# Opening an output projection with its ready tiles, and placing three root broadcasts later, in a two-layer decoder trunk

## The chip, the cores and the metric

The kernel runs on one core of one Trainium2 chip. The metric is the time of one execution on the device, in microseconds; less is better. It is written with a tile framework that places the semaphores. The order of TensorE's instructions is the order in which the program issues them; the other engines' orders are chosen by the framework's scheduler.

## The reference, cut to what matters

A trunk of two layers works on 528 tokens (16 meta tokens and 512 others) of width 1024, in float32. Each layer is a SwiGLU feed-forward block at half weight, a token mixer, and a second feed-forward block; layer 0 mixes by gated linear attention, layer 1 by sliding-window attention on a shared key/value set.

```python
def swiglu(x, w_in, w_out):
    gate, up = jnp.split(x @ w_in, 2, axis=-1)
    return (jax.nn.silu(gate) * up) @ w_out

# gated linear attention, end: o is the attention's output, (tokens, 4 heads, 256)
o = rmsnorm(o, g_head) * jax.nn.silu(r).reshape(B, L, GLA_HEADS, GLA_DV)
return o.reshape(B, L, GLA_V) @ w_out

# trunk, per layer
h = h + 0.5 * rmsnorm(swiglu(rmsnorm(h, g[0]), w_ffn_in[layer, 0], w_ffn_out[layer, 0]), g[1])
h = h + rmsnorm(mix, g[3])
h = h + 0.5 * rmsnorm(swiglu(rmsnorm(h, g[4]), w_ffn_in[layer, 1], w_ffn_out[layer, 1]), g[5])
```

The hidden width of a feed-forward block is 2816, that is 22 tiles of 128. Each head of the linear attention is normalized by its own root of mean square over its 256 channels.

## The kernel before

Activations lie transposed: 128 channels on the partitions, tokens along the free axis. Layer 0 works on two groups of tokens, of 272 and 256; most of layer 1's feed-forward work takes one group of 512. Each float32 operand is split into a high and a low part in a reduced format (ScalarE copies the high part, VectorE subtracts to get the low one), and each product is three matmuls: high by high, low by high, high by low (`mm3s`).

**A feed-forward block** (`ffn`) goes through its 22 hidden tiles in four chunks, of 4, 6, 6 and 6 (`FF_CHUNKS`). The first chunk is plain: `x_first` and `x_units` compute gate and up for four tiles, `evac` multiplies them and splits each into a pair tile `hid...` (L642 to L647, then L411 for the high and L412 for the low part). Then `out_proj` multiplies the four hidden tiles by the output weights: for each of eight output tiles m and each token group, four hidden tiles by three matmuls go into one PSUM bank `y`, which ScalarE copies to `Y` (L587). The later chunks use Strassen's scheme and begin their output projection early: `out_steps` is a generator that has a path for that, taken when it is given a list of `jobs` (evacuations still under way). There `begin` issues the matmuls of all hidden tiles but the last for the first output units, then the jobs are awaited, then `unit` adds the last hidden tile and evacuates. Meanwhile `right_factors` prepares the Strassen operands (`z...`, `xs...`) on ScalarE and VectorE.

**The linear attention** (`gla`) issues projections unit by unit through `x_units` (48 matmuls a unit with both groups), and between them the steps of one head at a time, `core(h, ...)`. A head begins when the head before it has ended: it waits for `cores[h - 1 : h]`. Its first step on TensorE transposes the values (`pv`). At its end the squares of its output are summed by matmuls with a vector of ones (`st_go`), GpSimd finds the reciprocal root by a chain of small operations and spreads it on a diagonal (`dg_go`, L387), two pairs of matmuls broadcast the diagonal to all partitions (`r_go`), and VectorE scales the head's output in `Y` (L987). This is `rstd`, called from `scale`, once per token group. The last eight projections are gates: `gated` (L1003 to L1010, then L411 and L412) needs the scaled output and makes the pair tiles `og`, which the attention's output projection reads; gates 0 and 1 wait for head 0, gates 2 and 3 for head 1, gates 4 to 7 for head 3.

**The order** is set by a planner, `Flow`. It keeps a clock that advances with each matmul by its columns over 2400 us (600 for plain float32). Side work is written as generators; `yield d` puts the rest of one back until the planner's clock has advanced by d, and it is issued when the matmuls of the main line have come that far (`flow.pump` after each product). So a number after `yield` says how many matmuls stand in TensorE's order between two steps. `rstd` yields `CHAIN + more` (5.0 plus what the caller asks for) between the sums and the broadcast; `BEHIND` is 2.2. `flow.wait(job)` issues side work until that job has ended.

**Weights** come by DMA on SyncE's queue into eight raw buffers; their splits go into the pool of 32 pair tiles (`SLOTS`), which also holds operands, hidden tiles and the tiles of the linear attention. `set_ahead` limits how many of them weights may hold; `done_w` gives them back when a unit of work has used them, and lets the next load go.

Of the kernel before, what the change touches and what calls it, by code (L numbers as in the profile page):

```python
# [46 lines left out]
BEHIND = 2.2  # L47
# [77 lines left out]
def trunk_kernel(ctx: ExitStack, tc, a, out):  # L125
    nc = tc.nc
    pe, act, dve, pool, sp = nc.tensor, nc.scalar, nc.vector, nc.gpsimd, nc.sync
    flow = Flow()
# [16 lines left out]
    def ps(name):  # L145
        return pp.tile([P, 512], F32, tag="ps", name=name)

    def pair_tile(name, dt=F32R):
        return hp.tile([P, 2, TOK], dt, tag="pair", name=name)

    def duo(name):
        t = pair_tile(name, F32)
        return t[:, 0], t[:, 1]
# [4 lines left out]
    def gain(layer, i, k):  # L158
        c = V_GAIN + layer * 48 + i * 8 + k
        return vec[:, c : c + 1]  # L160

    def mm(o, lhs, rhs, start=True, stop=True, onto=False):
        inst = pe.matmul(o, lhs, rhs, start=start, stop=stop, skip_group_check=onto)  # L163
        n = 1
        for d in rhs.shape[1:]:
            n *= d
        flow.clock += n / 2400 if rhs.dtype == F32R else max(n / 600, 0.12)
        return inst
# [41 lines left out]
    def set_ahead(n, slots=None):  # L210
        ahead[0], limit[0] = n, slots or n
        room[0].finish(flow)
        room[0] = Job(None)
# [138 lines left out]
    def rstd(sq, n, dim, half, name, eng=pool, more=0.0):  # L352
        c = 128 if n % 128 == 0 else n // 4
        nch = n // c
        st = ps(f"st_{name}")
        for j in range(nch):
            for i, t in enumerate(sq):
                mm(st[:c, j : j + 1], t[:, j * c : (j + 1) * c], ones[:, 0:1], i == 0, i == len(sq) - 1)
        av = sm.tile([P, 4], F32, tag="av", name=f"av_{name}")
        yv = sm.tile([P, 4], F32, tag="yv", name=f"yv_{name}")  # L360
        zv = sm.tile([P, 4], F32, tag="zv", name=f"zv_{name}")
        wv = sm.tile([P, 4], F32, tag="wv", name=f"wv_{name}")
        aa, yy, zz, ww = av[:c, :nch], yv[:c, :nch], zv[:c, :nch], wv[:c, :nch]
        if eng is dve:
            dve.tensor_scalar(aa, st[:c, :nch], 1.0 / dim, 1e-6, op0=ALU.mult, op1=ALU.add)
        else:
            act.activation(aa, st[:c, :nch], AF.Identity, scale=1.0 / dim, bias=eps[:c])
        eng.tensor_scalar(yy.bitcast(I32), aa.bitcast(I32), -0.5, RSQRT_MAGIC, op0=ALU.mult, op1=ALU.add)

        eng.tensor_tensor(zz, yy, yy, op=ALU.mult)  # L370
        eng.tensor_tensor(zz, zz, aa, op=ALU.mult)
        eng.tensor_scalar(ww, zz, 0.375, -1.25, op0=ALU.mult, op1=ALU.add)
        eng.tensor_tensor(ww, ww, zz, op=ALU.mult)
        if eng is dve:
            dve.scalar_tensor_tensor(yy, ww, 1.875, yy, op0=ALU.add, op1=ALU.mult)
            dve.tensor_tensor(zz, yy, yy, op=ALU.mult)
            dve.scalar_tensor_tensor(zz, zz, -0.5, aa, op0=ALU.mult, op1=ALU.mult)
            dve.scalar_tensor_tensor(yy, zz, 1.5, yy, op0=ALU.add, op1=ALU.mult)
        else:
            pool.tensor_scalar(ww, ww, 1.875, None, op0=ALU.add)  # L380
            pool.tensor_tensor(yy, yy, ww, op=ALU.mult)
            pool.tensor_tensor(zz, yy, yy, op=ALU.mult)
            pool.tensor_tensor(zz, zz, aa, op=ALU.mult)
            pool.tensor_scalar(zz, zz, -0.5, 1.5, op0=ALU.mult, op1=ALU.add)
            pool.tensor_tensor(yy, yy, zz, op=ALU.mult)
        dg = sm.tile([P, 272], F32, tag="dg", name=f"dg_{name}", bufs=2)
        eng.tensor_tensor(  # L387
            dg[:c, :n].rearrange("p (j c) -> p j c", c=c),
            (hident if half else ident)[:c, :c].unsqueeze(1).to_broadcast([c, nch, c]),
            yy.unsqueeze(2).to_broadcast([c, nch, c]),  # L390
            op=ALU.mult,
        )
        yield (DCHAIN if eng is dve else CHAIN) + more
        r = ps(f"r_{name}")
        mm(r[:, :n], ones[:c, :], dg[:c, :n])
        return r
# [12 lines left out]
    def split(dst, src, g):  # L409
        o, n = g  # L410
        act.activation(dst[:, 0, o : o + n], src, AF.Copy)  # L411
        dve.tensor_tensor(dst[:, 1, o : o + n], src, dst[:, 0, o : o + n].bitcast(F32), op=ALU.subtract)  # L412
# [142 lines left out]
    def out_proj(*args, **named):  # L555
        for _ in out_steps(*args, **named):
            pass
# [71 lines left out]
    def ffn(x, groups, finish, opening=False, tail=4):  # L629
        set_ahead(8 if opening else 16)  # L630

        def evac_to(hids):
            gss = {}

            def evac(i, g, p):
                o, n = g
                r = x.rt[:, o : o + n]
                if i % 2 == 0:
                    if i not in gss:
                        gss[i] = duo("gu")  # L640
                    gs = gss[i][0][:, o : o + n]
                    dve.tensor_tensor(gs, p[:, :n], r, op=ALU.mult)  # L642
                    act.activation(gs, gs, AF.Silu)
                else:
                    gs, us = (t[:, o : o + n] for t in gss[i - 1])
                    dve.tensor_tensor(us, p[:, :n], r, op=ALU.mult)
                    dve.tensor_tensor(us, gs, us, op=ALU.mult)  # L647
                    split(hids[i // 2], us, g)

            return evac  # L650

        jobs = []
        n2 = sum(n for _, n in groups) // 2
        halves = [(groups[0][0], n2), (groups[0][0] + n2, n2)]
        z, plain = {}, Job(None)

        def new_hid():
            hids.append(pair_tile(f"hid{x.name}_{lo + len(hids)}"))
            return hids[-1]

        for ci, (lo, hi) in enumerate(FF_CHUNKS):
            hids = []
            if ci == 0:
                jobs = x_first(x, 4, evac_to([new_hid() for _ in range(2)]), opening)
                set_ahead(16, 4)
                factors = flow.spawn(right_factors(x, halves, z, plain))
                for t in range(2, hi):
                    jobs += x_units(x, 2, groups, evac_to([new_hid()]))
                plain.finish(flow)
                set_ahead(16, 8)  # L670
            else:
                flow.wait(factors)
                set_ahead(16, RING)
                tiles = Strassen(z, halves)
                cur = tiles.head(new_hid())
                while cur:
                    last = len(hids) == hi - lo
                    if last:
                        fin = (finish, KD, True) if lo >= LAST else (None, 0, False)
                        proj = out_steps(hids, groups, x.groups, False, *fin, jobs)  # L680
                        end = used[0] + NLAST + tail
                    tiles.body(cur, (lambda: next(proj)) if last else (lambda: None))
                    nxt = None if last else tiles.head(new_hid())
                    jobs.append(tiles.tail(cur, last))
                    cur = nxt
            if ci == 0:
                flow.wait(*jobs)
                out_proj(hids, groups, x.groups, True)
                continue
            if lo >= LAST:  # L690
                set_ahead(32)
                cap[0] = min(end, len(units))
            for _ in proj:
                pass
# [121 lines left out]
    def gla(x, finish):  # L816
        set_ahead(10)
        with tc.tile_pool(name="gp", bufs=1) as gp:
# [61 lines left out]
            def core(h, before):  # L880
# [98 lines left out]
                accs = []  # L979
# [3 lines left out]
                        square_into(accs[gi], Y[:, 2 * h + i, o : o + n], i, 2, f"go{h}_{gi}")  # L983
                yield 2.0
                def scale(gi, o, n):
                    r = yield from rstd(accs[gi], n, 256, True, f"go{h}_{gi}", more=h // 3 * BEHIND)
                    dve.tensor_tensor(  # L987
                        yy[:, :, o : o + n], yy[:, :, o : o + n],
                        r[:, :n].unsqueeze(1).to_broadcast([P, 2, n]), op=ALU.mult,
                    )  # L990
# [32 lines left out]
            jobs = []  # L1023
# [208 lines left out]
    x = Operand("l0f0", lambda k: gain(0, 0, k), L0)  # L1232
# [51 lines left out]

    nxt, fin = into("l0m", 0, 1, True, lambda k: gain(0, 2, k), L0)
    ffn(x, L0, fin, True)
    x = nxt
    nxt, fin = into("l0f1", 0, 3, False, lambda k: gain(0, 4, k), L0)
    gla(x, fin)
    x = nxt  # L1290
    nxt, fin = into("kv", 0, 5, True, lambda k: vec[:, V_KVN + k : V_KVN + k + 1], L0)
    ffn(x, L0, fin, tail=8)


    with tc.tile_pool(name="kp", bufs=1) as kp:
        x = Operand("l1f0", lambda k: gain(1, 0, k), L1)
# [10 lines left out]
        x = nxt  # L1307
# [89 lines left out]
```

## Time and profile before

| what | value |
|---|---|
| median of 3 runs | 1932.98 us (1929.79 to 1935.67) |
| the profiled execution | 1932.53 us |
| its span, first to last instruction | 1930.5 us |
| mean granted TensorE clock | 0.992 of full speed |
| VectorE, ScalarE, GpSimd busy | 74%, 52%, 12% |
| DMA, mean over the span | 90 GB/s |

The profile is of one execution. A row of a timeline has the start in us, the length in us, the engine, the line of the kernel, the operation, what it writes and reads, the count of instructions merged in it, and in brackets the idle time of the engine before it with what ended it. PE is TensorE's matmuls, PEld its weight loads, which go ahead of the matmuls; DVE is VectorE, ACT ScalarE, POOL GpSimd, SP SyncE. A matmul of 272 columns in the reduced format follows the one before it after some 0.12 us, one of 512 columns after some 0.23 us. A row of the list of waits has who waited, for whom, the total in us, how often, and the longest. A row of a table of stretches has the stretch, its length, for each engine asked for the busy time and the count of instructions, then the granted clock, the DMA engines' share and GB/s.

Places in the span, in us: the four plain chunks' output projections begin at 60, 692, 1085 and 1610; the linear attention's roots stand at 466, 503, 542 and 581, and its output projection begins at 592.

### The profile page before, as it was taken

The page shows a single profiled execution, that of the slowest core. Times are in us where ns is not written, and L with a number is a line of the kernel's source. Part 1 is how long each engine was busy: PE and PEld are TensorE (multiplying, and loading weights), DVE is VectorE, ACT ScalarE, POOL GpSimd, SP SyncE. Part 2 cuts the span into 40 slices and gives each one's busy share as a digit, 9 for nine tenths or more (in the row PEclk, how much of TensorE's full clock was granted, in tenths as well). Part 3 has the DMA queues.
Part 4 walks back from the last instruction along what each step waited for, and adds up shares of the span by engine and source line. Part 5 has one row for each costly group of instructions (what it writes and reads, how often), then busy time and mean ns, then how long its engine had stood idle before and what let it go on. Part 6 is the DMA issues. An engine that isn't in the chain of part 4 may idle for free.

```text
span 1930.5 us, 37342 instructions
## 1 busy us (share of the span) xinstructions
PE 1889.1 (98%) x14502; PEld 1801.1 (93%) x14502; DVE 1419.5 (74%) x2868; ACT 1002.5 (52%) x2268; POOL 223.0 (12%) x417
## 2 busy tenths in 40 slices
PE   8999999999999999999999999999998999999997
PEld 8999999999999999999999798989975798989897
DVE  7885858765465798586887786868779678868584
ACT  5553535653245565353574553535646565536363
POOL 2000000321121300000034000000352040000002
PEclk9999999999999999999999999999999999999998
DMA  4223233322113122333351223233321212333331
GB/s 165 91 91 107 91 106 98 123 67 77 56 45 110 56 72 90 106 91 105 99 175 45 66 83 115 91 112 102 123 66 34 69 36 85 95 107 104 105 115 44
DMA packets 102016, 174.61 MB, mean 90 GB/s; under 512 B 11344, under 2 KB 24144, under 8 KB 101840
## 3 DMA queue, kind: packets, MB, share of 16 engines
q1 hardware_dynamic: 101008, 171.59, 28.4%
q8 instruction: 113, 1.85, 0.4%
q10 hardware_dynamic: 832, 0.65, 0.1%
q14 instruction: 63, 0.52, 0.1%
HBM read 170.10 MB, written 2.10 MB: 89 GB/s over the span
## 4 chain that ended last, share of the span: by engine, by line
PE 82%; DVE 12%; ACT 3%; issue 2%; POOL 1%; DMA 0%; SPq 0%; DVEq 0%; ACTq 0%
PE y L163 30%; PE a L163 18%; PE x L163 14%; PE c L163 8%; PE d L163 4%; DVE raw L252 1%; DVE w L228 1%; ACT w_s L246 1%; DVE w_s L247 1%; DVE w L247 1%; PE e L163 1%; PE o L163 1%; PE po L163 1%; DVE xsl0f L723 0%; PE ps L163 0%
## 5 line engine op out<-in xcount | busy, mean ns | idle before, releaser
L247 DVE TENSOR_TENSOR w_s<-raw,w_s 128x512 fp32r<-128x512 f32 x288 | 194.1, 691 | 132.9 <-ACT w_s L246 131.0
L163 PE MATMUL y<-hidl0f,w 128*128 128x272 f32 (+1 forms) x2112 | 264.8, 287 | 3.3 <-ACT hidl0f L411 3.1
L163 PEld LDWEIGHTS y<-hidl0f,w 128*128 128x128 f32 x2112 | 261.7, 190 | 4.4 <-ACT hidl0f L411 3.5
L228 DVE TENSOR_TENSOR w<-raw,w 128x512 fp32r<-128x512 f32 x378 | 243.2, 674 | 17.2 <-ACT w L227 15.4
L163 PE MATMUL y<-hidl1f,w 128*128 128x512 f32 (+1 forms) x1344 | 251.1, 346 | 1.7 <-ACT hidl1f L411 1.4
L246 ACT ACTIVATE w_s<-raw 128x512 fp32r<-128x512 f32 x288 | 175.3, 628 | 145.2 <-DVE raw L252 141.5
L163 PEld LDWEIGHTS y<-hidl1f,w 128*128 128x128 f32 x1344 | 212.3, 188 | 36.6 <-ACT hidl1f L411 2.3
L227 ACT ACTIVATE w<-raw 128x512 fp32r<-128x512 f32 x378 | 208.1, 586 | 35.4 <-PE y L163 27.0
L407 POOL TENSOR_TENSOR acc_post<-acc_post,sq_post 128x256 f32<-128x256 f32 (+1 forms) x72 | 59.1, 821 | 1376.7 <-ACT sq_post L406 1376.1
L252 DVE TENSOR_TENSOR raw<-raw,raw 128x512 f32<-128x512 f32 x288 | 198.3, 688 | 5.5
L247 DVE TENSOR_TENSOR w<-raw,w 128x512 fp32r<-128x512 f32 x216 | 148.6, 688 | 39.5 <-ACT w L246 38.8
L246 ACT ACTIVATE w<-raw 128x512 fp32r<-128x512 f32 x216 | 134.0, 621 | 48.0 <-PE y L163 47.7
L163 PE MATMUL x<-x_l0m,w 128*128 128x272 f32 (+1 forms) x1200 | 158.1, 288 | 0.0
L163 PEld LDWEIGHTS x<-x_l0m,w 128*128 128x128 f32 x1200 | 149.3, 189 | 1.1
L589 DVE TENSOR_TENSOR Y<-y,Y 128x256 f32<-128x256 f32 (+2 forms) x176 | 82.5, 474 | 72.0 <-PE y L163 71.5
L163 PE MATMUL a<-zl0f_t,w_s 128*128 128x264 f32 x864 | 117.3, 285 | 0.0
L163 PE MATMUL a<-zl1f_t,w_s 128*128 128x256 f32 x864 | 114.5, 281 | 0.3 <-ACT c L784 0.2
L163 PEld LDWEIGHTS a<-zl0f_t,w_s 128*128 128x128 f32 x864 | 110.1, 188 | 0.2
L163 PEld LDWEIGHTS a<-zl1f_t,w_s 128*128 128x128 f32 x864 | 107.3, 188 | 1.9 <-ACT c L784 1.5
L163 PE MATMUL x<-x_l0f,w 128*128 128x256 f32 (+1 forms) x768 | 100.4, 291 | 7.2 <-ACT w L227 5.8
L163 PEld LDWEIGHTS x<-x_l0f,w 128*128 128x128 f32 x768 | 97.0, 192 | 8.5 <-ACT w L227 5.8
L163 PE MATMUL x<-x_l1f,w 128*128 128x256 f32 (+1 forms) x576 | 92.7, 320 | 0.0
(483 smaller groups left out, 3308.7 us busy)
## 6 DMA issues: line engine op xcount, KB each, us to landing
raw<-in_w_in SPq DMA_DIRECT2D x352, 256.0 KB, 2.9
raw<-in_w_out SPq DMA_DIRECT2D x96, 256.0 KB, 3.4
raw<-in_gla_in SPq DMA_DIRECT2D x50, 256.0 KB, 2.9
raw<-in_w_last SPq DMA_DIRECT2D x48, 256.0 KB, 3.1
raw<-in_w_out SPq DMA_DIRECT2D x64, 128.0 KB, 2.9
raw<-in_gla_out SPq DMA_DIRECT2D x16, 256.0 KB, 2.7
raw<-in_w_q SPq DMA_DIRECT2D x16, 256.0 KB, 3.9
raw<-in_swa_out SPq DMA_DIRECT2D x16, 256.0 KB, 2.8
```

The costliest lines, as they stand in the source:

```text
L163: inst = pe.matmul(o, lhs, rhs, start=start, stop=stop, skip_group_check=onto)
L227: act.activation(w[:, 0, :m], raw[:, :m], AF.Copy)
L228: dve.tensor_tensor(w[:, 1, :m], raw[:, :m], w[:, 0, :m].bitcast(F32), op=ALU.subtract)
L246: act.activation(w[:, 0, :512], src, AF.Copy)
L247: dve.tensor_tensor(w[:, 1, :512], src, w[:, 0, :512].bitcast(F32), op=ALU.subtract)
L252: dve.tensor_tensor(dst, dst, src, op=ALU.add)
L407: pool.tensor_tensor(sums[0][:, :n], sums[0][:, :n], t[:, :n], op=ALU.add)
L589: dve.tensor_tensor(y, p[:, :n], y, op=ALU.add)
```

## The change

Two lines of use change. In the plain chunk the evacuations are handed to `out_proj` instead of being awaited ahead of it, so that the path with `begin` is taken. With two token groups it opens three output units (m = 0 for both groups, m = 1 for the first) with three hidden tiles each; with one group of 512 it opens two (m = 0 and m = 1). In the linear attention the root broadcast of heads 0, 1 and 2 gets the same extra 2.2 of the planner's clock that head 3 has already.

```diff
             if ci == 0:
-                flow.wait(*jobs)
-                out_proj(hids, groups, x.groups, True)
+                out_proj(hids, groups, x.groups, True, jobs=jobs)
                 continue
...
                 def scale(gi, o, n):
-                    r = yield from rstd(accs[gi], n, 256, True, f"go{h}_{gi}", more=h // 3 * BEHIND)
+                    r = yield from rstd(accs[gi], n, 256, True, f"go{h}_{gi}", more=BEHIND)
```

## The prediction, made before the result was known

> **What bounds the kernel.** I read the page first, then what the weight loads waited for, then the timelines around those waits. The page and the list of TensorE's waits:
>
> ```profile
> PE 1889.1 (98%) x14502; PEld 1801.1 (93%) x14502; DVE 1419.5 (74%) x2868; ACT 1002.5 (52%) x2268; POOL 223.0 (12%) x417
> ...
> PEld r_go L163 <- POOL dg_go L387: 6.4, 6, 2.6
> PEld y L163 <- ACT hidl0f L411: 3.5, 2, 2.7
> PEld y L163 <- ACT hidl1f L411: 2.3, 2, 1.2
> ```
>
> TensorE is busy 98% of the span, so a gain has to come out of its 41.4 us of idle time (1930.5 − 1889.1) or of its clock. The three waits shown are the ones that the two edits touch: the last hidden tile of the plain chunk (4 feed-forward layers) and the diagonal of the root (heads 0, 1, 2). Weight-load starts are the better ruler, because a matmul's modelled end hides part of each gap.
>
> **Part 1, plain chunk.** First layer: weight loads, then the ScalarE and VectorE work on the last hidden tile, then two stretches with the granted clock in the column behind the PE busy time.
>
> ```profile
> 59.94 1.18 PEld L163 LDWEIGHTS y<-hidl0f,w 128*128 128x128 f32 x9
> ...
> 64.59 6.50 PEld L163 LDWEIGHTS y<-hidl0f,w 128*128 128x128 f32 x33 [0.29 <-DVE hidl0f L412]
> ```
>
> ```profile
> 63.32 0.43 ACT L411 ACTIVATE hidl0f<-gu 128x272 fp32r<-128x272 f32 x1 [2.32 <-DVE gu L647]
> ...
> 64.18 0.40 ACT L411 ACTIVATE hidl0f<-gu 128x256 fp32r<-128x256 f32 x1
> ```
>
> ```profile
> 64.09 0.45 DVE L412 TENSOR_TENSOR hidl0f<-gu,hidl0f 128x272 fp32r<-128x272 f32 x1
> ...
> 65.04 0.43 DVE L412 TENSOR_TENSOR hidl0f<-gu,hidl0f 128x256 fp32r<-128x256 f32 x1
> ```
>
> ```profile
> 64.70:70.00 5.30, 5.30 (x24) 0.50 0.62 180
> 70.00:75.00 5.00, 5.00 (x43) 0.99 0.35 127
> ```
>
> Before, nine matmuls (three ready tiles by three products) run, then TensorE stands for the fourth tile. The nine loads start every (1.18 − 0.19)/8 = 0.124 us. The 44th load (9, then 2, then 33; two stand between the rows) starts at 64.59 + 6.50 − 0.19 = 70.90; undisturbed it would start at 59.94 + 43 × 0.1235 = 65.25. So 5.65 us are lost. Some of that is no wait: from 64.7 to 70.0 the clock is 0.50 and a matmul takes 5.30/24 = 0.221, so 24 × (0.221 − 0.1235) = 2.35 us of it is clock.
>
> After, 27 matmuls are ready before the fourth tile is needed (two groups of m = 0, one of m = 1). The 28th comes at 59.94 + 27 × 0.122 = 63.23 (those of 256 columns are a little shorter). It waits for the high part of group 0 (63.75, start 63.80: 0.57), the 30th for its low part (64.54: 0.56), the 33rd for the low part of group 1 (65.47: 0.58). Total 1.7 us, in three pieces. So the layer gains 5.65 − 1.7 = 4.0 us, if the clock stays up.
>
> The Trainium skill, "TensorE: Matmul & The Clock Gate", section "Why this matters for your kernels", asks for no idle gaps above about 3 us between bursts, or the clock falls back to half. The rows show 0.50 after a wait of 2.7 us, so the trace disagrees on the length; by the page's limit this layer would gain 5.65 − 2.35 − 1.7 = 1.6 and the sum below would be 10.4.
>
> What says that the pieces do not halve the clock: head 2 of the linear attention stands 2.61 + 0.55 us (rows further down) and the stretch around it keeps 1.00:
>
> ```profile
> 535.00:545.00 10.00, 7.48 (x57) 6.75 (x56) 6.22 (x11) 2.38 (x7) 7.38 (x22) 1.00 0.00 1
> ```
>
> So 2.7 us can halve it and 3.2 need not; 1.7 us is below both. The other layers, each by its first and a later row:
>
> ```profile
> 692.05 1.18 PEld L163 LDWEIGHTS y<-hidl0f,w 128*128 128x128 f32 x9
> 694.81 3.35 PEld L163 LDWEIGHTS y<-hidl0f,w 128*128 128x128 f32 x27 [0.47 <-DVE hidl0f L412]
> 695.25 0.44 DVE L412 TENSOR_TENSOR hidl0f<-gu,hidl0f 128x256 fp32r<-128x256 f32 x1
> 1084.93 2.05 PEld L163 LDWEIGHTS y<-hidl1f,w 128*128 128x128 f32 x9
> 1088.93 5.18 PEld L163 LDWEIGHTS y<-hidl1f,w 128*128 128x128 f32 x23 [0.43 <-DVE hidl1f L412]
> 1610.34 2.05 PEld L163 LDWEIGHTS y<-hidl1f,w 128*128 128x128 f32 x9
> 1614.18 5.86 PEld L163 LDWEIGHTS y<-hidl1f,w 128*128 128x128 f32 x26 [0.43 <-DVE hidl1f L412]
> ```
>
> The same sum gives: second layer, the 38th load at 697.97 instead of 692.05 + 37 × 0.1235 = 696.62, so 1.35; third, the 34th at 1093.92 instead of 1084.93 + 33 × 0.2325 = 1092.60, so 1.3; fourth, the 37th at 1619.85 instead of 1618.71, so 1.15. After, the second layer needs the low part of group 1 at 692.05 + 32 × 0.1235 = 696.0 and has it at 695.69; the third and fourth have one group of 512 columns, open two units, need the tile after 18 × 0.2325 = 4.2 us (1089.1, 1614.5) and have it at 1088.93 and 1614.18. All three waits go whole. Part 1: 4.0 + 1.35 + 1.3 + 1.15 = **7.8 us**.
>
> What it costs: no instruction is added. Three PSUM banks of eight are open at once; they are taken in the order in which they were taken before. Behind the waiting matmul on TensorE's queue stand only more output units. The weights of m = 0 are freed nine matmuls later (1.1 us, or 2.1 with 512 columns), and with them SyncE's loads and the splits for the first Strassen pair; the other seven output tiles, over 20 us of matmuls, hide that. Without that cover it would be 1.1 to 2.1 us a layer.
>
> **Part 2, roots.** Weight loads of heads 0, 1, 2 and 3. For head 3 the wait of 2.2 in the planner's clock is there already; the other three are to get it.
>
> ```profile
> 459.82 5.17 PEld L163 LDWEIGHTS x<-x_l0m,w 128*128 128x128 f32 x42
> 465.87 0.30 PEld L163 LDWEIGHTS r_go<-dg_go,ones 68*128 68x128 f32 x2 [0.89 <-POOL dg_go L387]
> ...
> 467.04 0.57 PEld L175 LDWEIGHTS pv<-ident,Y 128*128 128x128 f32 x4
> ```
>
> ```profile
> 497.05 5.17 PEld L163 LDWEIGHTS x<-x_l0m,w 128*128 128x128 f32 x42
> ...
> 504.62 0.57 PEld L175 LDWEIGHTS pv<-ident,Y 128*128 128x128 f32 x4
> ```
>
> ```profile
> 534.61 5.17 PEld L163 LDWEIGHTS x<-x_l0m,w 128*128 128x128 f32 x42
> 542.39 0.30 PEld L163 LDWEIGHTS r_go<-dg_go,ones 68*128 68x128 f32 x2 [2.61 <-POOL dg_go L387]
> 543.23 0.30 PEld L163 LDWEIGHTS r_go<-dg_go,ones 128*128 128x128 f32 x2 [0.55 <-POOL dg_go L387]
> 543.55 0.58 PEld L175 LDWEIGHTS pv<-ident,Y 128*128 128x128 f32 x4
> ```
>
> ```profile
> 573.56 7.72 PEld L163 LDWEIGHTS x<-x_l0m,w 128*128 128x128 f32 x63
> 581.21 0.77 PEld L163 LDWEIGHTS r_go<-dg_go,ones 68*128 68x128 f32 x4
> 582.02 10.37 PEld L163 LDWEIGHTS x<-x_l0m,w 128*128 128x128 f32 x84
> ```
>
> Head 3 has 63 projection matmuls in front of its roots, the others 42: the edit moves 21 matmuls ahead of the roots of each head. From the end of the projection loads to the next thing after the roots head 3 takes 582.02 − 581.28 = 0.74 us. Head 0 takes 467.04 − 464.99 = 2.05, head 1 504.62 − 502.22 = 2.40, head 2 543.55 − 539.78 = 3.77. Lost: 1.3, 1.65 and 3.0, together 6.0 us. With 63 in front the roots come 7.65 us after the first projection load (581.21 − 573.56): 467.5 and 504.7 for heads 0 and 1, past their diagonals; 542.26 for head 2, whose two diagonals are ready at 542.39 and 543.23: it still waits about 0.5. So 5.5 us go.
>
> Head 2's diagonal is late because GpSimd's chain is stretched beside VectorE's scan (1.25 us long):
>
> ```profile
> 537.09 1.15 POOL L373 TENSOR_TENSOR wv_go<-wv_go,zv_go 68x4 f32<-68x4 f32 x1
> ```
>
> The Trainium skill, "GPSIMD Engine Reference", section "Key points", has both engines share their SBUF interfaces when VectorE reads two inputs from there, which speaks against the edit: more cover does not shorten the chain. The 1.15 us agrees. Were all three heads stretched as head 2 is, each would keep 0.5 and the sum below would fall by 1.0.
>
> What is late next: a head starts when the head before it has scaled its output (at 467.04 head 1's transposes follow the roots at once). So head 1 moves 21 matmuls back in TensorE's order, head 2 42, head 3 63, with all that they issue on TensorE, VectorE, ScalarE and GpSimd; they issue no DMA. After head 3's roots 84 projection matmuls follow; 84 − 63 = 21 will be left, 2.6 us, before the output projection that needs all heads. VectorE then has this to do:
>
> ```profile
> 582.37 1.30 DVE L987 TENSOR_TENSOR Y<-Y,r_go 128x544 f32<-128x544 f32 x2
> 588.08 0.89 DVE L1010 SCALAR_TENSOR_TENSOR rg<-rg,vec,Y 128x272 f32<-128x272 f32 x2
> 592.28 0.78 DVE L1003 TENSOR_TENSOR rg<-x,R_l0m 128x272 f32<-128x272 f32 x2 [1.06 <-PE x L163]
> ```
>
> ```profile
> 595.47 8.65 PEld L163 LDWEIGHTS y<-og,w 128*128 128x128 f32 x71 [0.18 <-DVE og L412]
> ```
>
> The last gate already sets a wait of 0.18. New beside it: the scaling (1.30), gating tile 6 (0.89) and its two low parts (by the rows above 0.44 each, 0.88): 3.1 us of VectorE. The roots come 2.6 + 0.8 = 3.4 us ahead of the output projection, so most of it fits in front. Bounds: nothing, or all 3.1 us. I take 0.5, near the 0.18. Part 2: 5.5 − 0.5 = **5.0 us**.
>
> Sum 7.8 + 5.0 = 12.8 us. The profiled execution took 1932.5 (span 1930.5 and 2.0 around it), beside a median of 1933.0: **1920**.
>
> **Rivals.** *The clock still halves in the first layer.* The three pieces lie in a stretch of 2.3 us. For it: only 2.7 us did it before. Against: head 2's row. Price 2.35 us or a little more: 1922.5.
>
> *The last head comes too late.* For it: only 21 matmuls of cover are left. Against: the 3.4 us above. Price 3.1 instead of 0.5: 1922.6.
>
> *Only one edit works, or the gain is given back in queues that the scheduler orders anew* (VectorE and ScalarE are not ordered by hand, and head 2's chain hangs on what VectorE does beside it). Part 1 alone gives 1924.7, part 2 alone 1927.5; a halved stretch elsewhere would take 2.35 more.
>
> *Slower: tiles run out in the linear attention.* The pair pool has 32 tiles. By the code at head 3's state keys there are 8 of the operand, 8 weights, 3 for mask, resets and gates, the queries, 5 of the head, 3 outputs and a gate: 29. The edit puts that point a projection unit later, with one or two tiles more: 31. If I count two short, a weight split waits for a tile at the front of ScalarE's queue, with all evacuations behind it, until the head's next step, up to the 7.65 us of its longest. It decides from two such waits (15.3 against 12.8 won: 1935, still within 0.3%); three give 1942.7. Against it: today's projections wait for no weight in these stretches.
>
> **How the numbers follow.** Forecast 0.60; clock 0.10; late head 0.10; one edit or given back 0.12; tiles 0.08. The range: below, both waits go whole, 5.65 + 3.8 + 6.0 = 15.45, and another halved stretch with them, 17.8: 1914.7. Above, part 1 without its clock and part 2 with 3.1 in the tail, 5.45 + 2.4 = 7.85, and a halved stretch more, 5.5: 1927. I take 1914.5 to 1928. About 0.3% (5.8 us) is what a measurement of this kernel can tell from no change: faster takes the forecast, the clock, the late head and a little of the third (0.80); within, most of the third and a little of the tiles (0.12); slower, the rest (0.08).
>
> **What would show it.** After, the first y group has 27 loads (18 in the later two layers) and the waits of y on the hidden tiles fall to some 1.7 us, all in the first layer; the clock around 64 to 70 us is 1.00. Every head has 63 projection loads ahead of its roots; waits on the diagonal fall to about 0.5; 21 projection loads stand between the last roots and the output projection, and its wait on the gates stays below 1 us. I am wrong if a head keeps 42, if the output projection stands 3 us or more, or if projections begin to wait for split weights.

## The result and the profile after

The changed kernel takes 1918.5 us (median of 6 runs, 1917.3 to 1919.9) against 1931.4 for the kernel before (6 runs, 1929.8 to 1935.7): ratio 0.993, 95% interval 0.9917 to 0.9943, some 13 us. The forecast was 1920, from a sum of 12.8 us. The profiled execution took 1917.7, with a span of 1915.7.

First the page's line of the engines, then the list of what the weight loads waited for, of the changed kernel:

```profile
PE 1881.8 (98%) x14502; PEld 1797.4 (94%) x14502; DVE 1418.3 (74%) x2868; ACT 1002.1 (52%) x2268; POOL 219.5 (11%) x417
...
PEld a L163 <- ACT c L783: 2.5, 7, 0.9
PEld y L163 <- DVE hidl0f L412: 1.0, 2, 0.5
PEld y L163 <- ACT hidl0f L411: 0.5, 1, 0.5
PEld y L163 <- DVE og L412: 0.4, 1, 0.4
```

The waits on the diagonals (`r_go` on `dg_go`) are gone from the list, and so are those of layer 1's output units on the last hidden tile. Of layer 0's three short ones are left. The first line is new in size: 2.5 us, 0.9 in one piece; it comes up again below.

The first layer's weight loads, and the stretch of which the kernel before had half the clock (busy time of TensorE, weight loads, VectorE, ScalarE and GpSimd, then the clock):

```profile
59.31 3.37 PEld L163 LDWEIGHTS y<-hidl0f,w 128*128 128x128 f32 x27
63.17 0.30 PEld L163 LDWEIGHTS y<-hidl0f,w 128*128 128x128 f32 x2 [0.50 <-ACT hidl0f L411]
63.95 0.42 PEld L163 LDWEIGHTS y<-hidl0f,w 128*128 128x128 f32 x3 [0.49 <-DVE hidl0f L412]
64.89 7.23 PEld L163 LDWEIGHTS y<-hidl0f,w 128*128 128x128 f32 x59 [0.52 <-DVE hidl0f L412]
```

```profile
64.00:70.00 6.00, 5.68 (x45) 5.48 (x46) 6.00 (x11) 5.11 (x12) 0.00 (x0) 1.00 0.63 168
```

Twenty-seven loads in a row, then three waits of about half a microsecond, at the places that the forecast named, and the clock stays at 1.00. The other three layers run through without a break:

```profile
681.59 7.51 PEld L163 LDWEIGHTS y<-hidl0f,w 128*128 128x128 f32 x61
1073.17 8.95 PEld L163 LDWEIGHTS y<-hidl1f,w 128*128 128x128 f32 x39
1595.96 6.20 PEld L163 LDWEIGHTS y<-hidl1f,w 128*128 128x128 f32 x27
```

In the linear attention, head 2, and then head 3 with what follows it:

```profile
532.05 7.72 PEld L163 LDWEIGHTS x<-x_l0m,w 128*128 128x128 f32 x63
539.71 0.78 PEld L163 LDWEIGHTS r_go<-dg_go,ones 68*128 68x128 f32 x4
540.52 0.57 PEld L175 LDWEIGHTS pv<-ident,Y 128*128 128x128 f32 x4
```

```profile
570.53 7.73 PEld L163 LDWEIGHTS x<-x_l0m,w 128*128 128x128 f32 x63
578.20 0.78 PEld L163 LDWEIGHTS r_go<-dg_go,ones 68*128 68x128 f32 x4
579.00 2.71 PEld L163 LDWEIGHTS x<-x_l0m,w 128*128 128x128 f32 x21
581.64 3.00 PEld L163 LDWEIGHTS y<-og,w 128*128 128x128 f32 x23
585.09 5.00 PEld L163 LDWEIGHTS y<-og,w 128*128 128x128 f32 x41 [0.45 <-DVE og L412]
```

Sixty-three projection loads stand ahead of the roots, nothing waits for a diagonal, 21 loads are left behind the last roots, and the output projection waits 0.45 us for the last gate where it waited 0.18.

Where the time went, stretch by stretch, measured between starts of weight loads in the profiled executions (us). "Chunk" is from the first `y` load of the plain chunk to the first load of the next chunk; "attention" from the first value transposes (`pv`) to the output projection; "its end" from there to the second feed-forward block. The columns are the kernel before, the changed one, and the experiments e1 to e9:

```
                 before  after   e1     e2     e3     e4     e5     e6     e7     e8     e9
layer 1 chunk     29.08  25.05  25.04  26.66  29.23  25.04  27.32  23.97  25.04  23.98  28.18
attention        164.96 158.95 166.58 158.95 159.51 163.19 158.95 158.93 159.50 159.51 164.97
its end           48.60  48.83  48.58  48.86  48.44  50.52  48.86  48.88  48.42  48.37  48.60
layer 2 chunk     24.71  23.30  23.31  24.69  24.74  23.34  24.19  23.29  23.34  23.38  24.71
layer 3 chunk     23.59  22.20  22.26  23.61  23.56  22.23  22.20  22.22  22.24  22.21  23.59
layer 4 chunk     23.49  22.19  22.24  23.41  23.45  22.23  22.27  22.22  22.22  22.22  23.46
```

(Layers 1 to 4 here are the four feed-forward blocks in order.) Before to after: 4.0 + 6.0 − 0.2 + 1.4 + 1.4 + 1.3 = 13.9 us. The two spans differ by 14.8. The rest lies where neither edit is: 0.6 us ahead of the first output matmul, 1.3 in the stretch from layer 3's next chunk to the output projection of the sliding-window attention, which took 379 to 383 us in these eleven executions and has halved stretches of its own in each; and 0.9 back after layer 4.

That 0.9 is a new wait. In the changed kernel, then in the one before, the same product of the next chunk:

```profile
1625.06 1.13 PEld L163 LDWEIGHTS a<-zl1f_t,w_s 128*128 128x128 f32 x9 [0.93 <-ACT c L783]
```

```profile
1639.73 1.37 PEld L163 LDWEIGHTS a<-zl1f_t,w_s 128*128 128x128 f32 x11
```

TensorE's chunk begins 15.7 us earlier than before (1618.15 instead of 1633.83), but the ScalarE copy that it waits for ended at 1625.0 instead of 1639.7, 14.7 earlier. Ahead of that copy ScalarE stood for VectorE's sums of raw weights, in the changed kernel and in the one before:

```profile
1623.31 1.15 ACT L246 ACTIVATE w_s<-raw 128x512 fp32r<-128x512 f32 x2 [2.31 <-DVE raw L252]
1637.98 1.15 ACT L246 ACTIVATE w_s<-raw 128x512 fp32r<-128x512 f32 x2 [1.77 <-DVE raw L252]
```

VectorE goes through the same row of splits and Strassen operands in both, without a wait in the 11 us before these sums end, and 14.7 us earlier throughout: ScalarE and VectorE have become the later ones. The wait, of 0.8 or 0.9 us, stands in all seven profiles with the plain chunk's edit and in none of the four without it. The stretch from this chunk to the end of the kernel is longer than before by no more than that: by nothing in e4, by 0.9 in the changed kernel.

### The profile page after: what moved, and what is told of

Read it like the earlier page. It is cut to its first block, busy times and chain, and to the rows that moved or that the text cites. A ratio compares the mean times of both kernels' runs of the same rounds, so it can differ in the third digit from the quotient of the medians.

```text
span 1915.7 us, 37353 instructions
## 1 busy us (share of the span) xinstructions
PE 1881.8 (98%) x14502; PEld 1797.4 (94%) x14502; DVE 1418.3 (74%) x2868; ACT 1002.1 (52%) x2268; POOL 219.5 (11%) x417
## 4 chain that ended last, share of the span: by engine, by line
PE 79%; DVE 14%; ACT 4%; issue 2%; DMA 0%; POOL 0%; SPq 0%; DVEq 0%; ACTq 0%; POOLq 0%
PE y L163 29%; PE a L163 17%; PE x L163 16%; PE c L163 7%; PE d L163 4%; DVE raw L252 2%; ACT w_s L246 2%; DVE w_s L247 2%; DVE w L247 2%; DVE w L228 1%; PE o L163 1%; PE e L163 1%; PE po L163 1%; DVE hidl1f L808 1%; PE ps L163 0%
## 5 line engine op out<-in xcount | busy, mean ns | idle before, releaser
L163 PE MATMUL y<-hidl0f,w 128*128 128x256 f32 (+1 forms) x2112 | 261.9, 285 | 0.9 <-DVE hidl0f L412 0.6
```

## The experiments

The theory: both edits put ready matmuls where TensorE stood; a wait gives back what cover it gets, no more than its own length, and the two places add. The rivals: the gain is a matter of VectorE's and ScalarE's order, the moved heads are paid for at the end, and the clock plays no part.

**e1, the plain chunk alone.** Against the kernel before:

```diff
-                flow.wait(*jobs)
-                out_proj(hids, groups, x.groups, True)
+                out_proj(hids, groups, x.groups, True, jobs=jobs)
```

> Only the plain chunk is changed; the roots stay as before. Theory (the gain is the idle time of TensorE that ready matmuls fill, and the two edits add): 7.8 us less than before, 1923.6 against 1931.4, ratio 0.996; first layer back by 4.0 with the clock at 1.00 around 64 to 70 us, the others by 1.2 to 1.35 each, and the waits on the roots' diagonals stay at 6.4 us of weight-load idle. Rival (the gain comes from a new order of VectorE and ScalarE that needs both edits, or from the roots alone): within 2 us of 1931, or waits on the diagonals that change without their edit. Rival (the clock has no part): the first layer gives 1.6 instead of 4.0, together 5.4 us, 1926.0.

Measured: 1925.6 us against 1931.3 before, ratio 0.9967 (0.9955 to 0.9979), 5.7 us less. That is nearer to the 1926.0 of the rival that gives the clock no part than to the 1923.6 of the theory; the total does not tell them apart, the trace does. All four chunks have the lengths of the changed kernel, the first with its clock at 1.00, so the plain chunk gives its 4.0 us there and needs nothing of the other edit. In the profiled execution two things take from the 7.8: the 0.6 after layer 4, and head 2. Its weight loads and a stretch of TensorE right after it (busy time, count, clock):

```profile
537.84 0.30 PEld L163 LDWEIGHTS r_go<-dg_go,ones 68*128 68x128 f32 x2 [2.61 <-POOL dg_go L387]
```

```profile
539.10:542.40 3.30, 3.30 (x16) 0.50 0.02 5
```

The wait is the same 2.61 us as before the change, but here the clock was halved behind it, which the forecast's row of the kernel before (1.00) did not show. The attention took 1.6 us more than before.

**e2, the roots alone.** Against the kernel before:

```diff
-                    r = yield from rstd(accs[gi], n, 256, True, f"go{h}_{gi}", more=h // 3 * BEHIND)
+                    r = yield from rstd(accs[gi], n, 256, True, f"go{h}_{gi}", more=BEHIND)
```

> Only the roots of heads 0 to 2 are later; the plain chunk is as before. Theory: 6.0 us less than before, 1925.4, ratio 0.997; the linear attention from its first transposes to its output projection is 6.0 us shorter, all four heads have 63 projection loads ahead of the roots, no wait on a diagonal, and 21 projections stand ahead of the output projection, which waits about 0.45 for the gates. Rival (head 2 keeps 0.5 and the tail takes 0.5, as forecast): 5.0 us, 1926.4. Rival (the later heads are paid back at the output projection): 1930 to 1931.

Measured: 1924.0 us, ratio 0.996 (0.9947 to 0.9972), 7.2 us less; the attention is 6.0 shorter, to 0.01 us as in the changed kernel. 5.7 + 7.2 = 12.9, what both edits give together; each figure is good to some 2.4 us only, and the firmer sign that they add is that chunks and attention each have the changed kernel's lengths with one edit alone. The rival that the heads are paid back at the end falls. The profiled execution gains another 2.4 us in the first layer, which is not edited here: its weight loads, and the stretch from 64 to 70 us in e2 and in the kernel before (TensorE alone):

```profile
59.64 1.18 PEld L163 LDWEIGHTS y<-hidl0f,w 128*128 128x128 f32 x9
63.49 0.30 PEld L163 LDWEIGHTS y<-hidl0f,w 128*128 128x128 f32 x2 [2.67 <-ACT hidl0f L411]
```

```profile
64.00:70.00 6.00, 5.74 (x48) 1.00 0.63 186
```

```profile
64.00:70.00 6.00, 6.00 (x26) 0.50 0.55 159
```

The same wait, 2.67 against 2.68 us, and once 48 matmuls in six microseconds, once 26. The chunk takes 26.7 us without the halved clock and 29.1 with it.

**e3, the roots at half the distance, without the plain chunk's edit.** Its expectation names both edits; the kernel that ran had only this one, against the kernel before:

```diff
-                    r = yield from rstd(accs[gi], n, 256, True, f"go{h}_{gi}", more=h // 3 * BEHIND)
+                    r = yield from rstd(accs[gi], n, 256, True, f"go{h}_{gi}", more=(0.5 + h // 3 * 0.5) * BEHIND)
```

> Both edits, but heads 0 to 2 get half the extra distance (1.1 in the planner's clock; head 3 keeps 2.2), so that some 51 to 54 projections stand ahead of their roots, 6.2 to 6.6 us after the sums. Theory (a root needs only the cover that its diagonal takes): heads 0 and 1 wait 0.1 to 0.3 us each, as their diagonals came 6.0 and 6.4 us after the first projection load; head 2, if its GpSimd chain is stretched as before (7.8 us), waits 1.5, and if the chain is as short as in the changed kernel (6.2), nothing. Time 1918.7 to 1920.5. Rival (each microsecond of distance gives its share of the 6 us, whatever the chain): 3 us lost, 1921.5.

Measured: 1923.5 us, ratio 0.9957 (0.9941 to 0.9974); to be compared with e2's 1924.0 on the same chip, not with the changed kernel. The attention took 159.5 us, 0.56 more than with the whole distance. Half the distance gives nine tenths of the gain: the proportional rival falls.

**e4, twice the distance.** Against the changed kernel:

```diff
-                    r = yield from rstd(accs[gi], n, 256, True, f"go{h}_{gi}", more=BEHIND)
+                    r = yield from rstd(accs[gi], n, 256, True, f"go{h}_{gi}", more=(2 - h // 3) * BEHIND)
```

> Both edits, but heads 0 to 2 get twice the extra distance (4.4), some 84 projections ahead of their roots; head 3 keeps 2.2. Then 3 x 42 = 126 projections would have to come from the 84 that stood behind the last roots before: they run out, 21 stand ahead of head 3's roots and none behind. Theory (the move is free only while projections are left): TensorE waits some 4.4 us for head 3's diagonal (chain 6.9 us, cover 2.5), then 1.5 to 2 us for the last gates, and may lose 1.7 to 3.4 us to a halved clock: 1924.5 to 1928.5. Rival (the distance itself is free, the tail is hidden by the output projection's first matmuls): within 1 us of the changed kernel, 1918 to 1919.5.

Measured: 1924.9 us, ratio 0.9962 (0.9947 to 0.9977): 6 us lost again. The end of the attention, and TensorE around it:

```profile
578.49 2.62 PEld L163 LDWEIGHTS x<-x_l0m,w 128*128 128x128 f32 x21
584.67 0.50 PEld L163 LDWEIGHTS r_go<-dg_go,ones 68*128 68x128 f32 x2 [3.56 <-POOL dg_go L387]
585.52 0.56 PEld L163 LDWEIGHTS r_go<-dg_go,ones 128*128 128x128 f32 x2 [0.34 <-POOL dg_go L387]
586.17 9.99 PEld L163 LDWEIGHTS y<-og,w 128*128 128x128 f32 x63
```

```profile
584.00:590.80 6.80, 6.13 (x23) 0.50 0.17 58
```

As worked out, the projections run out: 21 ahead of the last roots, none behind. TensorE stands 3.6 + 0.3 us for the diagonal, and the clock is at half for 6.8 us from 584.0 on. Attention and its end take 5.9 us more than in the changed kernel. One part of the expectation failed: the wait of 1.5 to 2 us for the last gates does not come. The output projection's first 23 loads take 5.1 us at half the clock; the 24th, which needs the gate, comes at 591.25, just behind the gate's end at 591.16, and would have come some 2 us earlier at the pace of the changed kernel.

**e5, two open units instead of three in layer 0.** Against the changed kernel:

```diff
-            for m, g in order[1 : 2 if order[1][1][1] == SEQ else 3]:
+            for m, g in order[1 : 2 if order[1][1][1] == SEQ or first else 3]:
```

> Both edits, but layer 0's plain chunks open two output units instead of three (18 ready matmuls instead of 27); layer 1 as changed. Theory (ready matmuls fill the wait one for one): in the first layer the wait for the fourth tile's high part grows from 0.56 to 1.65 us, so about 1.1 us more, and if that brings the clock down to half (before, 2.7 us in one piece did) 2 to 2.4 more; in the second layer waits of 0.3 and 0.55 come back, 0.85. Time 1920.5 with the clock up, 1922.8 with it halved. Rival (the third unit is idle cover): 1918.5.

Measured: 1920.5 us, ratio 0.9949 (0.9934 to 0.9964): the number that the theory gave for a clock that stays up. But in the profiled execution (1920.4) the clock fell, so that this agreement is luck. The first layer:

```profile
59.53 2.25 PEld L163 LDWEIGHTS y<-hidl0f,w 128*128 128x128 f32 x18
63.39 0.30 PEld L163 LDWEIGHTS y<-hidl0f,w 128*128 128x128 f32 x2 [1.60 <-ACT hidl0f L411]
```

```profile
64.40:67.70 3.30, 3.25 (x14) 0.50 0.39 128
```

Nine matmuls fewer, 1.1 us more of waiting (1.60 instead of 0.50), and for 3.4 us the halved clock. The chunk is 2.3 us longer, 1.1 by waiting and 1.2 by the clock, where the theory had 2 to 2.4 for a halving; the second layer's is 0.9 longer: 3.2 in the trace, 2 in the medians. The third unit is no idle cover: it covers its own length, and in the profiled executions with it the clock stays up.

**e6, four open units in layer 0.** Against the changed kernel:

```diff
-            for m, g in order[1 : 2 if order[1][1][1] == SEQ else 3]:
+            for m, g in order[1 : 2 if order[1][1][1] == SEQ else 4 if first else 3]:
```

> Both edits, but layer 0's plain chunks open four output units (m = 0 and m = 1 for both groups, 36 ready matmuls; four PSUM banks open). Theory: of the first layer's three pieces of 0.56, 0.56 and 0.58 us only the last, for the low part of group 1, is left; 1.1 us less than the changed kernel, 1917.4; the other layers as they are. Rival (four open banks or the later release of weights cost something): 1918.5 or more, with new waits of y or of the next chunk's weights.

Measured: 1916.6 us, ratio 0.9934 (0.9917 to 0.9951). The first layer has one wait left:

```profile
59.84 5.07 PEld L163 LDWEIGHTS y<-hidl0f,w 128*128 128x128 f32 x41
65.42 4.70 PEld L163 LDWEIGHTS y<-hidl0f,w 128*128 128x128 f32 x38 [0.51 <-DVE hidl0f L412]
```

Its chunk takes 24.0 us, 1.1 less than with three units; the other chunks are unchanged. In the total 1 us cannot be told from none.

**e7, half the distance, with the plain chunk's edit.** Against the changed kernel, the edit of e3.

> Both edits, with half the extra distance for the roots of heads 0 to 2 (1.1). In the run of the roots alone at half the distance (the kernel of e3 did not have the plain chunk's edit, though its expectation named it) the linear attention took 159.5 us from its first transposes to its output projection, against 165.0 before and 158.95 with the whole distance, with 0.7 us of waits on diagonals left. Theory (cover beyond the diagonal's time is worth nothing, short of it a wait is left): the same 159.5 here, 0.55 more than the changed kernel, no slower after it: 1919.0. Rival (proportional): 162, 1921.5.

Measured: 1916.0 us, ratio 0.9923 (0.991 to 0.9935). The end of the attention:

```profile
576.13 0.30 PEld L163 LDWEIGHTS r_go<-dg_go,ones 128*128 128x128 f32 x2 [0.43 <-POOL dg_go L387]
576.45 6.00 PEld L163 LDWEIGHTS x<-x_l0m,w 128*128 128x128 f32 x48
582.38 5.75 PEld L163 LDWEIGHTS y<-og,w 128*128 128x128 f32 x45
```

The attention takes 159.5 us as expected, with 0.7 us of waits on diagonals in all. What the expectation missed: 48 projections are left behind the last roots instead of 21, the wait for the last gate goes, and the end is 0.4 us shorter (48.42 against 48.83). The median is 3.0 us below the 1919.0 that was expected; 0.4 of it is accounted for, and the intervals of the two kernels overlap. Half and whole distance can't be told apart in the total.

**e8, four open units and half the distance.** Against the changed kernel, the edits of e6 and e3.

> Four open output units in layer 0's plain chunks and half the extra distance for heads 0 to 2. Theory (the two places add): the first layer's chunk 24.0 us from its first output matmul to the next chunk, the linear attention 159.5, so 0.5 more than four units with the whole distance: 1917.1; a wait on the last gates of at most 0.2 instead of 0.45 gives back 0.3. Rival (the wait on the last gates is what limits, and less distance removes it): 1916.3 or less.

Measured: 1916.0 us, ratio 0.9918 (0.9904 to 0.9932), the lowest ratio of all. Chunk 23.98, attention 159.51, end 48.37: the three places add as expected. The total is the rival's (1916.3 or less) and not the theory's 1917.1, but the two are closer than this measurement can tell: beside e7 on the same chip it is no faster, and its interval overlaps that of the changed kernel.

**e9, the kernel before once more.**

> The kernel before, once more with its profile, to see whether the halved clock after the first layer's wait comes in each execution. Theory (the clock is judged in stretches of some 3.4 us that run on their own, so the same 2.7 us of waiting halves it or not by where they fall): either 29.1 us from the first output matmul to the next chunk with a halved stretch, or 26.7 without one; nothing between. Rival (the wait alone decides): 29.1 again, with a halved stretch.

Measured: 28.2 us for the first layer's chunk, between the two values that the theory allowed. The wait and the stretch behind it:

```profile
63.41 0.30 PEld L163 LDWEIGHTS y<-hidl0f,w 128*128 128x128 f32 x2 [2.68 <-ACT hidl0f L411]
```

```profile
65.50:68.90 3.40, 3.40 (x18) 0.50 0.72 189
```

Here the clock is halved too, but for 3.4 us, not 6.8, and it starts at 65.5 instead of 63.2. So "nothing between" was wrong; that the wait alone does not decide stands: 2.7 us of waiting cost no halving in e2, 3.4 us of it here, and 6.8 in the forecast's profile and in e3.

## Why the prediction was right

**The bound.** TensorE with its waits is where the 13 us came from: its two kinds of wait went and the spans followed. That the sum of 12.8 meets the measured 12.9 so closely is partly luck: single terms were off by 0.8 and 0.9 us in opposite directions, and one of 2.4 us belonged to the profiled execution and not to the kernel, as the next paragraphs show.

**Part 1, layers 2 to 4.** Forecast 1.35, 1.3 and 1.15; measured 1.4, 1.4 and 1.3. No wait is left on the tile.

**Part 1, layer 1.** Forecast 4.0, measured 4.0, with the three pieces of half a microsecond where they were put. But 2.4 of it was the clock, and that term belongs to the execution that was profiled: against e2's execution the same edit is worth 26.7 − 25.05 = 1.6. The step took the row with 0.50 for the kernel's, when it was one of three levels. That the three pieces would not halve the clock was argued from head 2's row at 1.00; the argument was weaker than it looked, since e1 shows that same wait with 0.50 behind it. The outcome held in all six profiled executions with three or four open units, and e5 shows how near it was: with one unit less the clock does fall.

The traces show what decided. In each of them the clock changes only at places that lie a whole multiple of 3.413 us apart (in the kernel before, 397 of these lengths from 63.25 to 1418.34), so each trace has a grid of its own, and a wait falls into one cell of it or into two. The cells in the first layer, TensorE alone, in the kernel before, in e9, in e2 and in the changed kernel:

```profile
59.84:63.25 3.41, 1.50 (x13) 1.00 0.41 142
62.07:65.48 3.41, 1.80 (x12) 1.00 0.00 0
62.26:65.68 3.42, 1.93 (x13) 1.00 0.00 0
62.47:65.89 3.42, 2.56 (x17) 1.00 0.05 8
```

By the rows of its matmuls TensorE is idle for 1.91, 1.61, 1.49 and 0.86 us of them. Behind the first two the clock is halved, behind the others not; in e2 the other 1.23 us of the wait lie in the cell before. Head 2 fits: its wait gave 1.13 and 1.39 us to two cells in the kernel before, and 2.33 to one in e1. In the eleven traces, from the first layer's chunk to the end of the linear attention, every cell at full clock with 1.6 us or more of idle time (six, 1.61 to 2.65) has a halved one behind it, and none with 1.5 or less has. The three pieces of the changed kernel come to 0.86 us by the same rows, wherever the grid lies; that, and not head 2's row, is why the step from them to a full clock was safe here.

By the Trainium skill, "TensorE: Matmul & The Clock Gate", section "Part 1: The HAM clock gate (the "warmup" mystery)", the clock is judged in free-running windows of about 3.4 us. The trace agrees: the halved stretches last 3.4 or 6.8 us and the same wait falls differently into them.

**What hides the later release of weights.** The step was that "the other seven output tiles, over 20 us of matmuls, hide that". As far as layer 4 shows, it held: counted from the chunk's first `y` load, VectorE's and ScalarE's work on the next weights does not come later in layer 4 than before (14.7 us earlier on the profile's scale, with a chunk that begins 14.4 earlier). What the forecast did not count is that this work is itself the limit there: TensorE comes 1.0 us sooner than it and gives 0.9 of the 1.3 us won back at a product of the next chunk.

**Part 2.** Forecast 6.0 of waits, of which head 2 would keep 0.5, and 0.5 lost at the end: 5.0. Measured 6.0 in the attention, and 0.2 lost at the end. The term that was mis-sized is head 2's 0.5: its diagonal was ready in time, because GpSimd's chain was stretched less: the second diagonal ended 7.7 us behind the first of the projection loads ahead of the roots, instead of 8.6. The operation that took 1.15 us beside the scan, and the scan itself, in the changed kernel:

```profile
533.78 0.39 POOL L373 TENSOR_TENSOR wv_go<-wv_go,zv_go 68x4 f32<-68x4 f32 x1
```

```profile
543.04 1.25 DVE L885 TENSOR_TENSOR_SCAN b<-resets,ls 128x528 f32<-128x528 f32 x1
```

The next head's scan now comes after the roots, at 543.0 instead of 537.0, and the chain ends earlier. In e1 and e9, where the scan stands beside the chain as before, that operation takes 1.15 us and TensorE waits 2.6 us; in e3 and e7, where it comes later, 0.20. So the forecast's cause of the late diagonal was right, and its step from it (more cover does not shorten the chain) missed that the edit would move the scan. The order is the scheduler's choice. The rest of the 0.8 us by which part 2 came out better is the tail, 0.2 instead of 0.5.

**The rivals.** The late head was a real limit, at another distance, and by another wait than the rival's: in e4 TensorE stands 3.9 us for the last diagonal and none for the gates, and with the halved clock that comes with it the price is 5.9 us, where the rival gave 2.6. Missing tiles did not show: no projection waits for a weight in the attention. The lines that cancel in the total are small: 0.8 us more from the roots, 0.3 more from the chunks, 0.9 back after layer 4.

## What to carry to other kernels

Work that is ready can be put ahead of a wait only as far as there is work: count the matmuls that the move takes from behind the last user (here 3 × 21 of 84; with 3 × 42 the roots' gain was gone). Cover a wait by its own length and leave the rest where it is; half the distance gave as much as the whole, as far as the totals tell. A wait on the matmul engine can cost twice, once in itself and once by the clock behind it. Whether it does differed here between executions with the same wait, by how the wait fell into cells of 3.41 us, so a term of clock read from one profile is given as a range.

## What was not expected of the hardware

A wait of 2.7 us in a stream of matmuls was followed by no halved clock (e2), by 3.4 us of it (e9) or by 6.8 us (before, e3), with 1.6 to 4.2 us between the lengths of the same chunk and the edited one. One of 1.6 us with 0.5 and 0.3 behind it was followed by 3.4 us (e5), three of half a microsecond by none (the changed kernel). In these places the halving followed the idle time that lay in one cell of the clock's grid of 3.41 us. It lasted two cells where the first halved cell still had 0.3 to 0.7 us of idle time in it (before, e3, e4), and one where it had 0.05 or less (e1, e5, e9). In the sliding-window attention of layer 1, with its smaller matmuls, the idle time of a cell does not separate the cases as well: a cell with 1.30 us was followed by a halved one (e5), and one with 1.70 was not (e9).
